# The last piece of an MLP's second matrix: seven products instead of eight for half of its columns, and one chunk of weights behind it

## The chip, the cores and the metric

The kernel runs on one core of a Trainium2 chip, in one launch. Its time is the device time in microseconds (us). Before the change three runs took 1203.53 us in the median (1203.21 to 1204.15). Five engines matter here: TensorE (PE, matrix products), VectorE (DVE) and ScalarE (ACT) for elementwise work, GpSimd (POOL) and SyncE (SP), which here only start transfers. Each engine works through its own instructions in the order in which the program holds them.

## The reference, cut to what matters

The kernel computes one layer of a decoder trunk for 256 tokens and 16 meta tokens, in float32. The change lies in its last part, the MLP:

```python
D_MODEL = 2048; SEQ = 256; D_FF = 8192
...
u = rms_norm(h, g_pre_mlp[l])
f = jnp.square(jax.nn.relu(u @ w_up[l])) @ w_down[l]
h = h + rms_norm(f, g_post_mlp[l])
return h[:, N_META:]
```

Call the activations A = relu(u @ w_up)^2 (256 tokens by 8192 features) and the weights B = w_down (8192 by 2048). The second matrix product is A @ B.

## The kernel before

**Pieces, halves, blocks.** The 8192 features are taken in NP = 8 pieces of 1024. Within a piece A falls into four blocks by token half t (128 tokens) and feature half h (512 features), and B into eight chunks by h and column block n (512 columns, n = 0 to 3). A chunk is 128 partitions by 4 by 512 numbers, 1 MB. Column blocks 2 and 3 ("X1" to "X4") are always computed plainly: each chunk is multiplied with the blocks of both token halves, and the sums stay in the PSUM banks `x00`, `x01`, `x10`, `x11` (column block, token half) over all pieces. Column blocks 0 and 1 (B11, B12, B21, B22) are computed by a scheme of seven products instead of eight (P1 to P7, the Strassen-Winograd form) in pieces 0 to 6. There each product takes one sum of B blocks and one sum of A blocks (a "form": A1 and A2 are the plain ones, S1 to S4 the sums). Its result lies in bank `a` or `b`, and `give` (L1697) adds it to one block of `F`, the sums of column blocks 0 and 1 in SBUF. In the last piece (i = NP - 1) these columns are computed plainly too, as Y1 to Y4.

**A product.** `down` (L1666 on) issues twelve matmuls of 512 columns, since each float32 number is split into a high and a low part: high by high, high by low, low by high, for four slices of the feature half.

**A chunk's way.** A 1 MB load on SP's queue brings it into one of five rooms (`raw_a`, `raw_c`, three `raw_m`; L1431). `split_raw` has ACT copy it to a high part (`hi`, L1475) and DVE subtract that to get the low part (`lo`, L1480). These parts have three slots in turn, so the split of a chunk starts only when the product three chunks earlier is done. A sum of two chunks is a DVE add in a room (L1496) or a load on POOL's queue that adds to what the room holds (`bring`, L1501). A room comes free after the last use of its chunk, and the next load waits for it.

**The order.** Everything is entered into a `Plan` with an engine, a cost and what it reads and writes. PE and SP keep the order of entry, and a slot of `hi` and `lo` is taken in turn. ACT and DVE take, of what can begin now, what is due first, by a due time worked back from the PE work that needs it; what no PE work needs has no due time and goes by entry. The order is fixed when the program is built. The PE order of the pieces is written out by hand; the last piece reads `Y1 U1b1 X1 Y3 Y2 Y4 X2 X3 X4`, where U1b1 is the last quarter of the product with w_up, from which the last activations come (`up_pair` L1545 on, `relu_squared`, `into_forms`).

**The end.** The last three chunks are not multiplied for both token halves in turn. After Y4 the code behind the loop runs X2, X3 and X4 for token half 0, then X2 for token half 1, then X3 and X4 for token half 1 in two column halves, into banks `a` and `b` (after a copy of `x11`, L1900). For each token half the output is F times g_post_mlp (`times_g`, L1883), the sum of squares on ACT (L969, in order of entry, as all write one scratch tile), a square root and a few small steps (`norm3`), and the last multiply-and-add with h1 (L1908), one per column stretch, each with its own output transfer.

```python
LAST_PIECE = "Y1 U1b1 X1 Y3 Y2 Y4 X2 X3 X4"
...
def last_of(w, s, t):
    h, n = AT[s]
    name, f = f"x{n - 2}{t}", (A1, A2)[t]
    plan.add("PE", 2.72, lambda: down(banks[name], split_at[w], h, f, False, h == 1),
             reads=half_names(w) + act_names(h, f), writes=(name,))
```

Of the kernel before, what the change touches and what calls it, by code (L numbers as in the profile page):

```python
# [14 lines left out]
P = 128  # L15
# [99 lines left out]
def hybrid_block(ctx: ExitStack, tc: tile.TileContext, ins: dict, out: bass.AP):  # L115
    nc = tc.nc
# [5 lines left out]
    NT = T // P  # L122
# [101 lines left out]
    NP = FF // PF  # L224
# [168 lines left out]
    for h in range(RH):  # L393
# [6 lines left out]
                        name=f"u_{tag}")[:, :, :, :L] for tag, n in (("um", KM), ("ux", KD - KM))], KM)  # L400
# [971 lines left out]
    NEXT = "X3 U0a0+ E2 U0a1+ X4 E1 P1 E3 E4 E5 U0b0+ P5 U0b1+ P3 P6 U1a0+ P7 U1a1+ P2 P4 U1b0+"  # L1372
    LAST_PIECE = "Y1 U1b1 X1 Y3 Y2 Y4 X2 X3 X4"
    steps = []
    for i in range(NP):
# [13 lines left out]

    BRINGS = {"P1": ("B11", "B12"), "E2": ("B12", "B22")}  # L1390

    SUMS_E = {"E1": ["T1"], "E3": ["T2", "T4", "T3"]}
    AT = {"B11": (0, 0), "B12": (0, 1), "B21": (1, 0), "B22": (1, 1),
          "Y1": (0, 0), "Y2": (1, 0), "Y3": (0, 1), "Y4": (1, 1),
          "X1": (0, 2), "X2": (1, 2), "X3": (0, 3), "X4": (1, 3)}
# [176 lines left out]
    def relu_squared(h, pr, i, s_name, box):  # L1572
# [17 lines left out]
        plan.add("ACT", 0.75, square, reads=(s_name,), writes=(s_name,))  # L1590
        if i < NP - 1 and h == 0:
            plan.add("ACT", 0.42, lambda: nc.scalar.copy(q_(S1Q), a_(A2)),
                     reads=(s_name,), writes=(f"q1{pr}",))
            plan.add("DVE", 0.42, lambda: nc.vector.tensor_sub(q_(S3Q), a_(A1), a_(A2)),
                     reads=(s_name,), writes=(f"q3{pr}",))
        elif i < NP - 1:
            plan.add("DVE", 0.42, lambda: nc.vector.tensor_sub(q_(S1Q), q_(S1Q), a_(A2)),
                     reads=(s_name, f"q1{pr}"), writes=(f"q1{pr}",))
            plan.add("DVE", 0.42, lambda: nc.vector.scalar_tensor_tensor(
                q_(S2Q), q_(S3Q), -1.0, a_(A2), op0=ALU.mult, op1=ALU.subtract),  # L1600
                reads=(s_name, f"q3{pr}"), writes=(f"q3{pr}",))
            plan.add("DVE", 0.42, lambda: nc.vector.tensor_add(q_(S4Q), a_(A1), q_(S2Q)),
                     reads=(s_name, f"q3{pr}"), writes=(f"q4{pr}",))
# [9 lines left out]
    def into_forms(h, pr, i, s_name, box):  # L1613
# [5 lines left out]
        def src():  # L1619
# [38 lines left out]
    for e, (s, i) in enumerate(steps):  # L1658
        if s[0] in "PEXY":
            last_reader[HALF_OF[s] if s in HALF_OF else AT[s][0], i] = e  # L1660
# [39 lines left out]
    def half_names(m_):  # L1700
        q = (first_n + m_) % 3
        return [f"hi{q}", f"lo{q}"]
# [18 lines left out]
    def product_plain(m_, s, i):  # L1721
        h, n = AT[s]
        for t, f in ((0, A1), (1, A2)):
# [4 lines left out]
                reads=half_names(m_) + act_names(h, f), writes=(name,))  # L1728


    LAST_BANK = {(0, 0): "a", (0, 1): "b", (1, 0): "u0", (1, 1): "u1"}

    def product_last(m_, s, i):
        h, n = AT[s]
        for t, f in ((0, A1), (1, A2)):
            name = LAST_BANK[n, t]
            plan.add("PE", 2.72, lambda t=t, f=f, name=name: down(
                banks[name], split_at[m_], h, f, h == 0, h == 1),
                reads=half_names(m_) + act_names(h, f), writes=(name,))
        for t in range(NT if h == 1 else 0):  # L1740
            name, blk = LAST_BANK[n, t], f"F{2 * t + n}"
            plan.add("DVE", 0.69, lambda t=t, name=name: nc.vector.tensor_add(
                F[:, t, n, :], F[:, t, n, :], banks[name]), reads=(name, blk), writes=(blk,))

# [88 lines left out]
    m_ = 0  # L1833
    tail = len(products) - 3
    for at_step[0], (s, i) in enumerate(steps):
# [17 lines left out]
        if s == "E3":  # L1853
            e3_at = m_
        {"U": product_up, "X": product_plain, "P": product_block, "Y": product_last,
         "E": product_e}[s[0]](m_, s, i)
# [131 lines left out]
```

## Time and profile before

| | |
|---|---|
| median of three runs | 1203.53 us |
| the profiled execution | 1202.46 us |
| its span in the profile | 1200.7 us |
| ACT busy | 650.9 us, 54% |
| POOL busy | 26.7 us, 2% |
| HBM read, written | 249.85 MB, 2.10 MB |

The span goes from the first to the last recorded instruction; the execution has 1.76 us around it. A row of the timeline gives the start in us from the start of the span, the duration, the engine, the line of the kernel, the operation, what it writes and reads, and in brackets how long the engine was idle before and on whom it waited. Since an instruction may start shortly before the one ahead of it on its engine has ended, what a row costs in a dense stretch is read from start to start. A row of the chain of waits gives the start, the time that this step took of the chain, and the engine and line.

### The profile page before, as it was taken

What the parts mean: (1) busy time and instruction counts of PE and PEld (TensorE: products, weight loads), DVE (VectorE), ACT (ScalarE), POOL (GpSimd) and SP (SyncE); (2) the same over time, 40 slices, a digit from 0 to 9 for tenths busy, and PEclk for the clock granted to TensorE, in tenths of its full rate; (3) what the DMA queues carried; (4) which work ended last, traced back from release to release, by engine and by line L of the source; (5) the groups of instructions that cost most, each with busy time, mean ns of one, the idle gap of its engine ahead of it and who ended that gap; (6) DMA issues with size and microseconds to landing.
All of it is one profiled execution on the core that took longest, in us unless ns stands there. A gap on an engine that the chain in (4) does not pass through costs nothing.

```text
span 1200.7 us, 16375 instructions
## 1 busy us (share of the span) xinstructions
PE 1191.2 (99%) x6694; PEld 1046.1 (87%) x6694; DVE 1015.0 (85%) x1128; ACT 650.9 (54%) x675; POOL 26.7 (2%) x37
## 2 busy tenths in 40 slices
PE   9999999999999999999999999999999999999997
PEld 9999988888888888898988888888889889888886
DVE  6899978999676778688898888898988988988966
ACT  6533344343584455666566565655665665565543
POOL 1000000000000000000000000000000000000000
PEclk9999999999999999999999999999999999999999
DMA  9655555556558578547777777786896787777851
GB/s 294 208 184 183 186 184 188 198 188 198 182 168 284 171 258 265 178 156 230 205 243 222 205 252 206 211 274 158 243 275 165 253 245 199 245 223 197 257 176 70
DMA packets 170043, 253.01 MB, mean 211 GB/s; under 512 B 4369, under 2 KB 92625, under 8 KB 169456
## 3 DMA queue, kind: packets, MB, share of 16 engines
q1 hardware_dynamic: 160000, 230.64, 58.6%
q0 software_dynamic: 9072, 20.08, 8.9%
q8 instruction: 52, 0.85, 0.3%
q10 hardware_dynamic: 896, 1.25, 0.3%
q14 instruction: 23, 0.19, 0.0%
HBM read 249.85 MB, written 2.10 MB: 210 GB/s over the span
## 4 chain that ended last, share of the span: by engine, by line
PE 99%; DVE 0%; DVEq 0%; ACT 0%; issue 0%; ACTq 0%
PE bank_u L485 18%; PE acc_gate L771 15%; PE bank_u L491 9%; PE acc_up L1673 8%; PE bank_a L1673 7%; PE o_c L1110 6%; PE bank_b L1673 6%; PE acc_z L480 4%; PE acc_co L771 4%; PE acc_po L771 4%; PE bank_b L1758 3%; PE acc_v L480 3%; PE acc_g L480 3%; PE acc_up L1758 3%; PE acc_vg L480 2%; PE acc_up L485 1%
## 5 line engine op out<-in xcount | busy, mean ns | idle before, releaser
L485 PE MATMUL bank_u<-m,hi 128*128 128x512 f32 x960 | 332.5, 391 | 0.0
L491 PE MATMUL bank_u<-m,lo 128*128 128x256 f32 x960 | 266.7, 278 | 0.0
L274 ACT CAST hi<-raw 128x2048 fp32r<-128x2048 f32 (+2 forms) x94 | 151.2, 1619 | 192.0 <-PE acc_gate L771 67.7
L1480 DVE TENSOR_TENSOR lo<-raw_m,hi 128x2048 fp32r<-128x2048 f32 (+1 forms) x98 | 208.8, 2137 | 44.6 <-ACT hi L1475 44.2
L1475 ACT CAST hi<-raw_m 128x2048 fp32r<-128x2048 f32 (+1 forms) x98 | 174.8, 1788 | 132.0 <-PE bank_u L485 61.8
L277 DVE TENSOR_TENSOR lo<-raw,hi 128x2048 fp32r<-128x2048 f32 (+2 forms) x94 | 180.1, 1925 | 40.5 <-ACT hi L274 39.9
L485 PEld LDWEIGHTS bank_u<-m,hi 128*128 128x128 f32 x960 | 180.3, 188 | 38.0
L491 PEld LDWEIGHTS bank_u<-m,lo 128*128 128x128 f32 x960 | 180.8, 188 | 1.4
L771 PE MATMUL acc_gate<-hi,u_um 128*128 128x512 f32 x416 | 131.5, 390 | 0.0
L546 DVE SCALAR_TENSOR_TENSOR c<-a,taps,c 128x256 f32<-128x256 f32 x240 | 115.6, 483 | 6.8
L771 PEld LDWEIGHTS acc_gate<-hi,u_um 128*128 128x128 f32 x416 | 78.1, 188 | 16.2
L1673 PE MATMUL acc_up<-hi,forms 128*128 128x512 f32 x272 | 86.8, 391 | 0.0
L1475 ACT CAST hi<-raw_c 128x2048 fp32r<-128x2048 f32 (+1 forms) x34 | 61.3, 1807 | 43.9 <-PE bank_u L485 24.5
L1480 DVE TENSOR_TENSOR lo<-raw_c,hi 128x2048 fp32r<-128x2048 f32 (+1 forms) x34 | 73.5, 2164 | 12.8 <-ACT hi L1475 12.7
L1480 DVE TENSOR_TENSOR lo<-raw_a,hi 128x2048 fp32r<-128x2048 f32 (+1 forms) x32 | 70.0, 2189 | 15.8 <-ACT hi L1475 15.8
L1475 ACT CAST hi<-raw_a 128x2048 fp32r<-128x2048 f32 (+1 forms) x32 | 58.5, 1832 | 44.6 <-PE bank_u L485 16.3
L1673 PE MATMUL bank_a<-hi,forms 128*128 128x512 f32 (+1 forms) x256 | 82.0, 383 | 0.0
L771 PE MATMUL acc_gate<-lo,u_um 128*128 128x512 f32 x208 | 80.9, 389 | 0.0
L1110 PE MATMUL o_c<-hi,m 128*128 128x512 f32 x208 | 65.5, 390 | 0.0
L1673 PE MATMUL bank_b<-hi,forms 128*128 128x512 f32 (+1 forms) x200 | 64.0, 383 | 0.0
L1673 PEld LDWEIGHTS acc_up<-hi,forms 128*128 128x128 f32 x272 | 51.1, 188 | 11.1
L1673 PEld LDWEIGHTS bank_a<-hi,forms 128*128 128x128 f32 x256 | 47.7, 188 | 9.5
(383 smaller groups left out, 2181.1 us busy)
## 6 DMA issues: line engine op xcount, KB each, us to landing
raw<-in_w_in_dram SPq DMA_DIRECT2D x52, 1024.0 KB, 5.1
raw_m<-in_w_down_dram SPq DMA_DIRECT2D x38, 1024.0 KB, 6.3
raw_m<-in_w_up_dram SPq DMA_DIRECT2D x37, 1024.0 KB, 6.0
raw_c<-in_w_down_dram SPq DMA_DIRECT2D x14, 1024.0 KB, 5.3
raw_a<-in_w_down_dram SPq DMA_DIRECT2D x12, 1024.0 KB, 6.0
raw_a<-in_w_up_dram SPq DMA_DIRECT2D x11, 1024.0 KB, 6.1
raw_o<-in_w_o_dram SPq DMA_DIRECT2D x10, 1024.0 KB, 7.1
raw_c<-in_w_up_dram SPq DMA_DIRECT2D x10, 1024.0 KB, 6.0
```

The source lines that it names most:

```text
L274: nc.scalar.copy(hi[:, sl, cs], raw[:, sl, cs])
L277: nc.vector.tensor_sub(lo[:, sl, cs], raw[:, sl, cs], f32(hi[:, sl, cs]))
L480: nc.tensor.matmul(acc, w[:, k[0], cs], act[:, k[1], a, off:], start=first and n == 0, stop=last and n == 2)
L485: nc.tensor.matmul(acc.rearrange("p (a t) -> p a t", a=2)[:, :, ts], hi[:, k[0], cs], act[:, k[1], :, off + ts.start:off + ts.stop], start ...
L491: nc.tensor.matmul(acc[:, :T], lo[:, k[0], cs], act[:, k[1], 0, off:], start=False, stop=stop, skip_group_check=True)
L546: nc.vector.scalar_tensor_tensor(c, conv["a"][:, q, i:i + T], taps[:, q, i:i + 1], c, op0=ALU.mult, op1=ALU.add)
L771: nc.tensor.matmul(acc, act(kk)[:, a_, ts_], w_[:, k, :], start=kk == 0 and n == 0, stop=kk == nk - 1 and n == 2)
L1110: nc.tensor.matmul(acc, form(k, a_), box[w_][:, k, :], start=start and k == 0 and n == 0, stop=stop and k == CK - 1 and n == 2, skip_group ...
L1475: nc.scalar.copy(box["hi"][:, ks, cs], raw[:, ks])
L1480: nc.vector.tensor_sub(box["lo"][:, ks, cs], raw[:, ks], f32(box["hi"][:, ks, cs]))
L1673: nc.tensor.matmul(acc, forms[h][:, f, k, a_, :], box[w_][:, k, cs], start=start and k == 0 and n == 0, stop=stop and k == KH - 1 and n == ...
L1758: nc.tensor.matmul(banks[bank][:, col_halves[half[1]]], forms[h][:, f, k, a_, :], split_at[m_][w_][:, k, cs], start=start and k == 0 and n ...
```

## The change

In the last piece column blocks 0 and 1 go by the seven products too. The PE order becomes `P1 U1b1 X1 X2 P5 X3 P6 P3 P7 P2 P4 X4`, and only X4 is left for the code behind the loop: X4 for token half 0, then X4 for token half 1 in two column halves. X2 and X3 are multiplied for both token halves inside the loop. The sums of A blocks (S1 to S4) are made in the last piece as in the others, and the sums of B chunks as well; where the other pieces add B22 to B12 at E2, the last piece, which has no E steps, does it at X3. `product_last` with its banks goes.

```diff
-    LAST_PIECE = "Y1 U1b1 X1 Y3 Y2 Y4 X2 X3 X4"
+    LAST_PIECE = "P1 U1b1 X1 X2 P5 X3 P6 P3 P7 P2 P4 X4"
...
-    BRINGS = {"P1": ("B11", "B12"), "E2": ("B12", "B22")}
+    BRINGS = {"P1": ("B11", "B12"), "E2": ("B12", "B22"),
+              ("X3", NP - 1): ("B12", "B22")}
...
-            if s in BRINGS:
-                to, what = BRINGS[s]
+            if (s, i) in BRINGS or s in BRINGS:
+                to, what = BRINGS.get((s, i)) or BRINGS[s]
...
-        if i < NP - 1 and h == 0:
+        if h == 0:
             plan.add("ACT", 0.42, lambda: nc.scalar.copy(q_(S1Q), a_(A2)),
...
-        elif i < NP - 1:
+        else:
             plan.add("DVE", 0.42, lambda: nc.vector.tensor_sub(q_(S1Q), q_(S1Q), a_(A2)),
...
-        if i == NP - 1:
-            return
...
-    def product_last(m_, s, i):
...
-    tail = len(products) - 3
+    tail = len(products) - 1
...
-    last_of(m_, "X2", 0)
     before_last(0)
-    ends = [(m_ + 1, "X3"), (m_ + 2, "X4")]
-    for w, s in ends:
-        last_of(w, s, 0)
+    last_of(m_, "X4", 0)
...
-    last_of(m_, "X2", 1)
     before_last(1)
...
     for e, cs in enumerate(col_halves):
-        for w, s in ends:
-            h = AT[s][0]
-            plan.add("PE", 1.36, lambda w=w, h=h, e=e, cs=cs: down(
-                banks["ab"[e]][:, cs], split_at[w], h, A2, False, h == 1, cs),
-                reads=half_names(w) + act_names(h, A2), writes=("ab"[e],))
+        plan.add("PE", 1.36, lambda e=e, cs=cs: down(
+            banks["ab"[e]][:, cs], split_at[m_], 1, A2, False, True, cs),
+            reads=half_names(m_) + act_names(1, A2), writes=("ab"[e],))
```

More of the change, by code (lines that the diff above doesn't have):

```diff
@@ L1388, in hybrid_block @@
     SUM_FOR = {"P6": ("B11", "B22"), "P4": ("B11", "B21")}
-    BRINGS = {"P1": ("B11", "B12"), "E2": ("B12", "B22")}
+    BRINGS = {"P1": ("B11", "B12"), "E2": ("B12", "B22"),
+              ("X3", NP - 1): ("B12", "B22")}
     SUMS_E = {"E1": ["T1"], "E3": ["T2", "T4", "T3"]}
     AT = {"B11": (0, 0), "B12": (0, 1), "B21": (1, 0), "B22": (1, 1),
-          "Y1": (0, 0), "Y2": (1, 0), "Y3": (0, 1), "Y4": (1, 1),
           "X1": (0, 2), "X2": (1, 2), "X3": (0, 3), "X4": (1, 3)}
@@ L1658, in hybrid_block @@
     for e, (s, i) in enumerate(steps):
-        if s[0] in "PEXY":
+        if s[0] in "PEX":
             last_reader[HALF_OF[s] if s in HALF_OF else AT[s][0], i] = e
@@ L1728, in product_plain @@
                 reads=half_names(m_) + act_names(h, f), writes=(name,))
-    LAST_BANK = {(0, 0): "a", (0, 1): "b", (1, 0): "u0", (1, 1): "u1"}
-    def product_last(m_, s, i):
[L1734 to L1743, printed above, removed]
     def product_block(m_, s, i):
@@ L1854, in hybrid_block @@
             e3_at = m_
-        {"U": product_up, "X": product_plain, "P": product_block, "Y": product_last,
+        {"U": product_up, "X": product_plain, "P": product_block,
          "E": product_e}[s[0]](m_, s, i)
```

## The prediction

> **What bounds the kernel now.** I read the page first (who is busy), then the chain of waits of the last 60 us (what sets the end), then VectorE's and ScalarE's timelines there, then transfers.
>
> ```profile
> PE 1191.2 (99%) x6694; PEld 1046.1 (87%) x6694; DVE 1015.0 (85%) x1128; ACT 650.9 (54%) x675; POOL 26.7 (2%) x37
> ```
>
> TensorE is without gaps; VectorE has 15% left over the kernel. The last piece in the chain of waits (the rows of U1b1, which lie between the first two here, left out):
>
> ```profile
> 1143.02 2.74 PE bank_a L1673 x12
> ...
> 1153.94 5.46 PE acc_up L1673 x24
> ...
> 1164.85 2.72 PE bank_a L1673 x12
> ...
> 1175.73 10.88 PE acc_up L1673 x48
> 1186.61 2.87 PE bank_a L1673 x24
> 1189.48 2.89 PE bank_b L1673 x24
> ```
>
> Twelve matmuls are 2.72 us; the same in two column halves half of 2.87 + 2.89, so 2.88. Y1 starts at 1143.02 and TensorE ends at 1192.37: sixteen products' worth at 2.72, two at 2.88, and a few hundredths. From there an end that TensorE has no part in runs to 1200.7. VectorE's timeline, from which all its prices come:
>
> ```profile
> 1123.51 2.29 DVE L1496 TENSOR_TENSOR raw_a<-raw_a,raw_c 128x2048 f32<-128x2048 f32 x1
> 1125.76 2.29 DVE L1480 TENSOR_TENSOR lo<-raw_c,hi 128x2048 fp32r<-128x2048 f32 x1
> 1127.97 0.68 DVE L1697 TENSOR_TENSOR F_raw<-F_raw,bank_a 128x512 f32<-128x512 f32 x1
> ...
> 1137.14 2.29 DVE L1480 TENSOR_TENSOR lo<-raw_m,hi 128x2048 fp32r<-128x2048 f32 x1
> ...
> 1139.95 0.68 DVE L1697 TENSOR_TENSOR F_raw<-F_raw,bank_a 128x512 f32<-128x512 f32 x1
> 1140.55 2.28 DVE L1480 TENSOR_TENSOR lo<-raw_m,hi 128x2048 fp32r<-128x2048 f32 x1
> ...
> 1158.40 0.69 DVE L1622 TENSOR_TENSOR forms<-pairs,forms 128x512 fp32r<-128x512 f32 x1
> ...
> 1166.83 2.29 DVE L1480 TENSOR_TENSOR lo<-raw_m,hi 128x2048 fp32r<-128x2048 f32 x1 [3.15 <-ACT hi L1475]
> ...
> 1171.05 0.43 DVE L1900 COPY bank_b<-acc_up 128x256 f32<-128x256 f32 x1
> 1171.39 0.68 DVE L1883 TENSOR_TENSOR F_raw<-F_raw,raw_m 128x512 f32<-128x512 f32 x1
> ...
> 1185.31 0.15 DVE L947 SCALAR_TENSOR_TENSOR v_mlp<-ssq_mlp,v_mlp 128x1 f32<-128x1 f32 x1
> ...
> 1186.57 0.75 DVE L1908 SCALAR_TENSOR_TENSOR F_raw<-F_raw,r_mlp,h 128x512 f32<-128x512 f32 x1
> ...
> 1188.04 0.15 DVE L938 TENSOR_REDUCE v_mlp<-ssq_mlp 128x1 f32<-128x3 f32 x1
> ...
> 1188.29 0.74 DVE L1908 SCALAR_TENSOR_TENSOR F_raw<-F_raw,r_mlp,h 128x512 f32<-128x512 f32 x1
> 1188.95 0.75 DVE L1908 SCALAR_TENSOR_TENSOR raw_m<-raw_m,r_mlp,h 128x512 f32<-128x512 f32 x1
> ...
> 1190.09 0.42 DVE L1943 TENSOR_TENSOR raw_m<-bank_a,raw_m 128x256 f32<-128x256 f32 x1 [0.39 <-ACT sq_last L1942]
> ...
> 1190.68 0.74 DVE L1908 SCALAR_TENSOR_TENSOR raw_m<-raw_m,r_mlp,h 128x512 f32<-128x512 f32 x1
> ...
> 1192.96 0.42 DVE L1943 TENSOR_TENSOR raw_m<-bank_b,raw_m 128x256 f32<-128x256 f32 x1 [1.53 <-ACT sq_last L1942]
> ...
> 1194.01 1.42 DVE L1908 SCALAR_TENSOR_TENSOR F_raw<-F_raw,r_mlp,h 128x384 f32<-128x384 f32 x2
> 1195.34 1.54 DVE L1908 SCALAR_TENSOR_TENSOR raw_m<-raw_m,r_mlp,h 128x512 f32<-128x512 f32 x3
> ```
>
> From start to start: a sum of two chunks 2.25; a low part 2.21; a `give` 0.60 (1139.95 to 1140.55), which I also take for `times_g` (same operation and size); a bank copy 0.34; `finish` 1.26; `start` 0.25; the end of a column half 0.59 and 1.05; an output step 0.66; the last five output steps 2.87 (1194.01 to 1196.88). After 1196.88 there are 3.82 us to the end: last transfers. Today token half 0 is finished (four output steps, the last at 1190.68) while TensorE still works.
>
> **What is removed.** Seven products for eight leave TensorE seventeen for eighteen, and of the split ones one remains: minus 2.88 us. Without stalls, in the chain's clock: P1 1143.02, U1b1 1145.77, X1 1151.22, X2 1156.68, P5 1162.12, X3 1164.84, P6 1170.28, P3 1173.00, P7 1175.72, P2 1178.44, P4 1181.16, X4 for half 0 1183.88, its halves 1186.60 to 1189.49.
>
> **What is added.** Three splits (twelve chunks for nine), sums for P6 and P4, two adding loads, sums of A blocks and their S1 to S4, seven `give` for four adds at L1742. The part up to X2 has room: P1 stands where Y1 stood, with the same chunk and slot, and the sums of A blocks made before it are those that every earlier piece makes there under a full TensorE. They cost nothing; if that cover went, each would cost its 0.60.
>
> **X2, moved forward.** It needs the forms of U1b1 and now starts 5.46 us after U1b1's end; Y2 had two chunks between. The steps as they ran before on ScalarE, U1b1 ending at 1153.94 in the chain:
>
> ```profile
> 1153.98 0.37 ACT L1552 COPY half<-bank_u 128x256 f32<-128x256 f32 x1 [2.35 <-PE bank_u L491]
> 1154.25 1.91 ACT L1475 CAST hi<-raw_m 128x2048 fp32r<-128x2048 f32 x1
> 1156.06 0.63 ACT L1582 ACTIVATE pairs<-pairs 128x512 f32<-128x512 f32 x1
> 1156.72 0.62 ACT L1621 CAST forms<-pairs 128x512 fp32r<-128x512 f32 x1
> ...
> 1164.88 1.91 ACT L1475 CAST hi<-raw_m 128x2048 fp32r<-128x2048 f32 x1 [3.53 <-PE bank_u L1673]
> ```
>
> The low form ended at 1158.40 + 0.69 = 1159.09, 5.15 us after U1b1, with a split ahead of it on both queues. That is 0.31 us early, and S1 to S4 are due later. X2's stall is bounded by 0 and by what P5's split, which takes the place of that split, can wait for its adding load:
>
> ```profile
> DMA to landing us min/median/max: 8.3/9.4/14.2
> ```
>
> That load starts when P1's low part is done, 1137.14 + 2.21 = 1139.35, as for Y1; median landing 1148.8, latest 1153.6. ScalarE gets to P5's split at 1151.5 and would hold the square behind it. By the median the stall is 0, by the latest 2.1 less 0.3, so 1.8. I take 0.
>
> **The run of products on VectorE.** A split starts when the product three chunks earlier ends; its low part starts 1.95 us later (1164.88 to 1166.83). Before X2's end VectorE has had all that is ready: the sum for P6, S1 to S4, X3's split. Then, each start the later of "high part ready" and "VectorE free": P6 low part 1164.10 (X2's end + 0.03 + 1.95), `give` P5 1166.31, P3 low 1166.91, sum for P4 1169.12 to 1171.37; P7 low must wait for X3's end, 1172.26 (0.89 idle); `give` P6 1174.47, P2 low 1175.07, `give` P3 1177.28, P4 low 1177.88, `give` P7 1180.09, X4 low 1180.69, `give` P2 1182.90 to 1183.50. Each low part is in time, and so is each `give` whose bank is written next: P6's by 1175.07 for P7 at 1175.72, P3's by 1177.88 for P2 at 1178.44, P7's by 1180.69 for P4 at 1181.16. The least margin is 0.47 us, so I put no stall on TensorE. But VectorE is full.
>
> **The end.** Where Y4 had X2, X3 and X4 behind it, the last F blocks are now whole only with P2 and P4. ScalarE squares each block ahead of its `times_g`, in order of entry, 0.75 apart:
>
> ```profile
> 1177.62 0.62 ACT L969 ACTIVATE ng_offset=None)_1_0_9569<-F_raw 128x512 f32<-128x512 f32 x1
> ...
> 1178.37 0.63 ACT L969 ACTIVATE ng_offset=None)_0_1_9585<-F_raw 128x512 f32<-128x512 f32 x1
> ```
>
> The first waits for `give` P2; from 1183.55 six squares end at 1184.30, 1185.05 and so on to 1188.05, each within hundredths of its `times_g` or ahead of it. VectorE: copy 0.34 to 1183.84; P4 ends at 1183.88, so `give` P4 1183.93 to 1184.53, the other copy to 1184.87 (both before the halves at 1186.60); five `times_g` to 1187.87; `start` 1188.12; `times_g` for X4's half 0 1188.72; `finish` 1189.98; `times_g` and `start` for half 1 1190.83; column half ends 0.59 and 1.05 to 1192.47, both of TensorE's long done; four output steps 2.64 to 1195.11; five 2.87 to 1197.98. With 3.82 behind: 1201.80, 1.10 us over 1200.7. What stood under three chunks of TensorE stands behind it: VectorE's work, not TensorE's end, sets the end.
>
> Gains of VectorE are bounded: without its idle 0.89 and 0.09 the end would be 1200.82, level with before. So no step of the order can earn the 2.88.
>
> **Transfers.** g_post_mlp's load waited for a room; P1's room is now held until P4, so the load moves behind P3's split, 1169.12.
>
> ```profile
> raw_m<-in_g_post_mlp_dram SPq DMA_DIRECT2D x1, 1024.0 KB, 4.5
> ```
>
> It lands at 1173.6, 11 us before use: free, under the splits. On SP's queue only it stands behind X4's load. The outputs of both halves now come in one go; their bytes, and the stretch in which the last ones go out today:
>
> ```profile
> HBM read 249.85 MB, written 2.10 MB: 210 GB/s over the span
> ```
>
> ```profile
> 1196.00:1198.00 2.00, 0.00 (x0) 0.00 (x0) 0.88 (x3) 0.00 (x0) 0.00 (x0) 0.50 0.87 327
> ```
>
> At 327 GB/s for a share of 0.87, full engines move 376 GB/s, and 2.10 MB takes 5.6 us. The outputs are issued over 1193.1 to 1198, about the same rate. Bounds: 0, if the queue keeps up; 0.7, if the whole 5.6 us runs before the last output's usual end starts to count (5.6 less the 4.9 of issue). I take 0.4, being near the edge.
>
> Sum: 1.10 + 0.4 = +1.5 us on the span, 1202.2. The profiled execution's 1202.46 (1.76 around the span) lies 1.07 below the median; I add the difference to the median: 1205.0.
>
> A rule weighed: two low parts in a row start 2.21 us apart though each row lasts 2.29. The Trainium skill, "VectorE: DVE Perf Modes", section "The DRAIN you can't avoid", says that the next operation does not start until the pipe is empty (and excepts, further on, one that is not held). Taken plainly, the 27 longer operations from 1172.26 on would each cost 0.08 more, an estimate of +2.2 us on top of the sum. The rows contradict it, so the sum keeps 2.21.
>
> **Rivals.** *TensorE alone counts* (chance 0.04). Everything new hides, as in pieces 0 to 6, and the time falls by 2.88 to 1200.65. For it: 99% busy, and scheme pieces without gaps. Against it: there U products of 5.44 us alternate with the P's, while here five P's stand in a row at 2.72 us with 2.21 + 0.60 of VectorE each. The Trainium skill, "Perfetto Trace Analysis", section "Identifying the Most-Contended Engine", would say this: optimize the engine with the highest occupancy first (it warns that matmul busy time flatters). It agrees with the row of 99%, and is not enough at the end.
>
> *X2 waits for its forms* (0.16): the adding load lands late, ScalarE's queue holds the square, 1.8 us of stall, after which VectorE's chain moves by as much: +3.3, 1206.8. It decides from a landing over 12.5 us after issue; the longest was 14.2, the median speaks against it.
>
> *A `give` behind a split* (0.17), the slower side: DVE's order puts a low part ahead of the `give` of the bank that the next product writes. TensorE then stands for 2.21 less the margin of about 0.5, so 1.7, and slots come free later, which VectorE pays as idle time. At two of the places P7, P2, P4: +3.4, in all +4.9, 1208.4. It decides from 0.47 us of lateness. Due times speak against it, the thin margin for it.
>
> *VectorE packs better* (0.05): no idle time, +0.5, 1204.0.
>
> **How the numbers follow.** The forecast itself has 0.58; its own range is 1203.6 (the gapless end) to 1206.3 (0.3 more of transfers, a microsecond of waits not seen). The whole range, 1203.3 to 1207.9, takes in the late load and leaves out the first rival and two thirds of the third, some 0.16. Below 0.2% (2.4 us) this kernel can't tell a change from none. Faster by more: 0.04. Slower by more than that, over 1205.9: both slower rivals, 0.33, and 0.11 of the forecast's own upper part, 0.44. Within: 0.52.
>
> **What would show it.** Right: TensorE's last matmul near 1189.5 with hardly a gap; VectorE without a gap over 0.9 us from 1164 to 1198; output steps of half 0 after the last column half; a longer stretch from TensorE's end to the span's end, near 12.7 instead of 8.3. X2 waiting for `forms`, or P7, P2, P4 for L1697, shows the rivals. Wrong would be an end after TensorE still near 8.3 us, or gaps in TensorE of over 2 us before 1162.

## The result and the profile after

| | before | after |
|---|---|---|
| median of 12 runs | 1203.49 us | 1206.22 us |
| lowest, highest | 1202.69, 1204.24 us | 1205.71, 1207.64 us |
| profiled execution, its span | 1202.46, 1200.7 us | 1205.85, 1204.1 us |

The ratio after to before is 1.0024, interval 1.0017 to 1.0032: 2.7 us slower, where 1205.0 us had been predicted with a range of 1203.3 to 1207.9. The spans differ by 3.4 us. Of these, 0.72 were there before the last piece began: P1 starts at 1143.74 in the chain of waits of after, where Y1 started at 1143.02. What is compared below is compared from there on, and there it is 60.36 us to the end for 57.68, so 2.68 us, as in the medians.

The busy line and the chain's shares on the page of after:

```profile
PE 1189.2 (99%) x6670; PEld 1042.9 (87%) x6670; DVE 1032.3 (86%) x1148; ACT 659.9 (55%) x684; POOL 29.2 (2%) x39
...
PE 97%; DVE 2%; DMA 0%; issue 0%; ACT 0%; SPq 0%; DVEq 0%; ACTq 0%
```

TensorE has 24 matmuls fewer and is still 99% busy; VectorE has 20 instructions and 17.3 us more. The shares hardly move. The chain of waits of after shows what did, in the last 45 us:

```profile
1143.74 2.75 PE bank_a L1671 x12
...
1151.94 10.92 PE acc_up L1671 x48
1162.88 1.93 ACT hi L1475
1164.83 2.29 DVE lo L1480
...
1176.61 2.98 PE bank_a L1671 x12
1179.59 2.80 PE bank_b L1671 x12
1182.39 2.81 PE bank_a L1671 x12
1185.23 0.70 DVE F_raw L1695
```

Before, this chain stayed on TensorE until its last matmul. Now it leaves TensorE at the end of X2 (1162.88) and goes by VectorE; P7, P2 and P4 are on it, but as links that wait for a `give` (L1695). From 1185.23 it never comes back to TensorE, though that works on until 1190.78. Behind TensorE's end lies this window (length, then the busy time and instructions of TensorE, weight loads, VectorE, ScalarE, GpSimd, then clock, DMA share and GB/s), first of before, then of after:

```profile
1192.40:1200.70 8.30, 0.00 (x0) 0.00 (x0) 3.81 (x10) 0.77 (x3) 0.00 (x0) 0.68 0.42 156
```

```profile
1190.80:1204.10 13.30, 0.00 (x0) 0.00 (x0) 8.94 (x26) 1.87 (x8) 0.00 (x0) 0.69 0.45 159
```

TensorE's end came 1.6 us sooner on each trace's own clock, and 5.0 us more lie behind it, nearly all of it VectorE's work (8.94 for 3.81 us).

TensorE's timeline of after, at the seams of the products (P5's first matmul, the last of P3 and the first of P7, the first of P2 and X4):

```profile
1162.68 0.39 PE L1671 MATMUL bank_b<-hi,forms 128*128 128x512 f32 x1
...
1176.05 0.39 PE L1671 MATMUL bank_b<-hi,forms 128*128 128x512 f32 x1
1176.61 0.47 PE L1671 MATMUL bank_a<-hi,forms 128*128 128x512 f32 x1 [0.16 <-DVE F_raw L1695]
...
1179.43 0.45 PE L1671 MATMUL bank_b<-hi,forms 128*128 128x512 f32 x1
...
1185.03 0.39 PE L1671 MATMUL acc_up<-hi,forms 128*128 128x512 f32 x1
```

Eight products' worth at 2.72 us from 1162.68 would put X4 at 1184.44; it starts at 1185.03, so 0.59 late. P7 is 0.33 late (P3's next matmul slot was 1176.28), and then each product takes 2.80 or 2.82. VectorE's timeline of after says why:

```profile
1167.04 0.68 DVE L1636 TENSOR_TENSOR forms<-F_raw,forms 128x512 fp32r<-128x512 f32 x1
...
1169.84 0.42 DVE L1602 TENSOR_TENSOR F_raw<-pairs,F_raw 128x256 f32<-128x256 f32 x1
...
1172.98 0.68 DVE L1636 TENSOR_TENSOR forms<-F_raw,forms 128x512 fp32r<-128x512 f32 x1
1173.58 2.28 DVE L1480 TENSOR_TENSOR lo<-raw_m,hi 128x2048 fp32r<-128x2048 f32 x1
1175.78 0.68 DVE L1695 TENSOR_TENSOR F_raw<-F_raw,bank_a 128x512 f32<-128x512 f32 x1
1176.38 2.28 DVE L1480 TENSOR_TENSOR lo<-raw_a,hi 128x2048 fp32r<-128x2048 f32 x1
1178.58 0.68 DVE L1695 TENSOR_TENSOR F_raw<-F_raw,bank_b 128x512 f32<-128x512 f32 x1
...
1185.23 0.69 DVE L1695 TENSOR_TENSOR F_raw<-F_raw,bank_a 128x512 f32<-128x512 f32 x1 [0.37 <-PE bank_a L1671]
...
1186.62 1.89 DVE L1866 TENSOR_TENSOR F_raw<-F_raw,raw_c 128x512 f32<-128x512 f32 x3
...
1189.92 0.16 DVE L938 TENSOR_REDUCE v_mlp<-ssq_mlp 128x1 f32<-128x3 f32 x1 [0.22 <-ACT ng_offset=None)_2_0_9665 L969]
...
1190.64 0.69 DVE L1866 TENSOR_TENSOR raw_m<-acc_up,raw_c 128x512 f32<-128x512 f32 x1 [0.37 <-ACT ng_offset=None)_3_0_9680 L969]
...
1194.75 1.41 DVE L1891 SCALAR_TENSOR_TENSOR F_raw<-F_raw,r_mlp,h 128x512 f32<-128x512 f32 x2
...
1198.72 1.53 DVE L1891 SCALAR_TENSOR_TENSOR raw_m<-raw_m,r_mlp,h 128x512 f32<-128x512 f32 x3
```

A low part and a `give` together take 2.80 us from start to start (1173.58 to 1176.38), a product 2.72. The `give` at 1175.78 ends at 1176.46 and P7 starts 0.15 later; those of 1178.58 and 1181.38 end at 1179.26 and 1182.06, and P2 and P4 start 0.17 behind each. From P7 on, TensorE goes at VectorE's pace. Behind 1185.23 lies one long queue of VectorE: copies, factors, roots, and from 1194.75 nine output steps, the last done at 1200.25. After that 3.85 us pass to the end, 3.82 before.

### The profile page after: what moved, and what is told of

The parts are those of the page before. It is cut to its first block, busy times and chain, and to the rows that moved or that the text cites. A ratio compares the mean times of both kernels' runs of the same rounds, so it can differ in the third digit from the quotient of the medians.

```text
span 1204.1 us, 16371 instructions
## 1 busy us (share of the span) xinstructions
PE 1189.2 (99%) x6670; PEld 1042.9 (87%) x6670; DVE 1032.3 (86%) x1148; ACT 659.9 (55%) x684; POOL 29.2 (2%) x39
## 4 chain that ended last, share of the span: by engine, by line
PE 97%; DVE 2%; DMA 0%; issue 0%; ACT 0%; SPq 0%; DVEq 0%; ACTq 0%
PE bank_u L485 18%; PE acc_gate L771 14%; PE bank_u L491 9%; PE acc_up L1671 7%; PE bank_a L1671 7%; PE o_c L1110 6%; PE bank_b L1671 5%; PE acc_z L480 4%; PE acc_co L771 4%; PE acc_po L771 4%; PE bank_b L1741 3%; PE acc_v L480 3%; PE acc_g L480 3%; PE acc_up L1741 3%; PE acc_vg L480 2%; PE acc_up L485 1%
## 5 line engine op out<-in xcount | busy, mean ns | idle before, releaser
L1475 ACT CAST hi<-raw_m 128x2048 fp32r<-128x2048 f32 (+1 forms) x101 | 180.5, 1792 | 132.1 <-PE bank_u L485 69.2
L1480 DVE TENSOR_TENSOR lo<-raw_m,hi 128x2048 fp32r<-128x2048 f32 (+1 forms) x101 | 215.6, 2141 | 38.5 <-ACT hi L1475 38.2
L1671 PE MATMUL acc_up<-hi,forms 128*128 128x512 f32 x280 | 89.4, 391 | 0.0
L1671 PE MATMUL bank_a<-hi,forms 128*128 128x512 f32 (+1 forms) x264 | 86.0, 387 | 0.2 <-DVE F_raw L1695 0.2
```

Source lines behind the costliest of these rows:

```text
L1475: nc.scalar.copy(box["hi"][:, ks, cs], raw[:, ks])
L1480: nc.vector.tensor_sub(box["lo"][:, ks, cs], raw[:, ks], f32(box["hi"][:, ks, cs]))
L1671: nc.tensor.matmul(acc, forms[h][:, f, k, a_, :], box[w_][:, k, cs], start=start and k == 0 and n == 0, stop=stop and k == KH - 1 and n == ...
```

## The experiments

The theory of the prediction, called A in the expectations: VectorE's queue behind the last `give` sets the end, with ScalarE's chain of squares close behind it. Against it stood A' (VectorE alone, ScalarE never in the way), B (TensorE or its inputs are late), C (the added work of the scheme costs the time, not the shortened cover) and D (only the length of the cover counts). The interval of a ratio is about 0.001 to each side, some 1.1 us, so single steps are read from the traces, and the times decide between theories that lie further apart. Each ratio is to the kernel before as it ran beside that row (medians of 1203.09 to 1203.49 us), so the ratios compare better than the medians. One measure returns below: from the start of `give` P4 to the first output step, 9.52 us in after (1185.23 to 1194.75). It is left blank where the run has no P4 or other products stand between the two.

| run | median us | ratio to before, interval | `give` P4 to the first output step on VectorE |
|---|---|---|---|
| after | 1206.22 | 1.0024, 1.0017 to 1.0032 | 9.52 |
| e1_no_factor | 1204.76 | 1.0012, 1.0003 to 1.0021 | 8.22 |
| e2_factor_twice | 1208.56 | 1.0044, 1.0031 to 1.0056 | 11.93 |
| e3_cover_alone | 1206.01 | 1.0024, 1.0015 to 1.0034 | |
| e5_two_behind | 1207.38 | 1.0035, 1.0022 to 1.0047 | |
| e4_squares_ready | 1205.52 | 1.0017, 1.0008 to 1.0025 | 8.74 |
| e6_factor_pool | 1205.00 | 1.0013, 1.0004 to 1.0022 | 8.26 |
| e7_pool_ready_act | 1203.76 | 1.0002, 0.9994 to 1.0011 | 7.09 |
| e9_outputs_too | 1204.57 | 1.0008, 1.0000 to 1.0017 | 9.29 |
| e10_forms_early | 1205.81 | 1.0020, 1.0011 to 1.0029 | 9.52 |
| e12_outputs_after_root | 1204.69 | 1.0011, 1.0003 to 1.0020 | 7.08 |
| e14_all_moves | 1204.08 | 1.0006, 0.9997 to 1.0015 | 7.04 |
| e15_all_but_outputs | 1203.36 | 0.9999, 0.9991 to 1.0008 | 7.03 |

### Less and more of VectorE's work behind the last product

Four of the eight factors with g_post_mlp (column blocks 0 and 1 of both token halves) are left out (e1_no_factor), or made twice, one of the two copies into a free room (e2_factor_twice).

```diff
-        plan.add("DVE", 0.69, lambda: nc.vector.tensor_mul(
+        plan.add("DVE", 0.69, lambda: n < 2 or nc.vector.tensor_mul(
```

> The changed kernel with four VectorE instructions left out: the products of F (column blocks 0 and 1, both token halves) with g_post_mlp, so these columns come out without that factor; the order of everything else is kept. Theory A (behind the last give, VectorE's queue sets the end, with ScalarE's chain of squares close behind it): 4 x 0.60 = 2.4 us of VectorE go, but the factor for X4's token half 0 cannot start before its square ends, which is seven squares after P2's give, about 1189.4 in the profile's clock instead of 1190.6; so about -1.2 us against the changed kernel, 1.0014 of the kernel before. Theory A' (VectorE's queue alone): -2.4 us, 1.0004. Theory B (the loss comes from TensorE, through X2's early place, the adding loads or stalls between the products): no change, 1.0022 to 1.0024.

```diff
+    spare = room_of[free_rooms[0]][:, :CW]
...
-        plan.add("DVE", 0.69, lambda: nc.vector.tensor_mul(
-            dst_of(t, n * CW, (n + 1) * CW), src, g_mlp[:, block(n)]),
+        def f():
+            if n < 2:
+                nc.vector.tensor_mul(spare, src, g_mlp[:, block(n)])
+            nc.vector.tensor_mul(dst_of(t, n * CW, (n + 1) * CW), src, g_mlp[:, block(n)])
+        plan.add("DVE", 0.69, f,
```

> The changed kernel with the same four VectorE products done twice, the first time into an unused room; the output is the reference's. Theories A and A': 4 x 0.60 = 2.4 us more in VectorE's queue behind the last give, all of it on the path: +2.4 us, 1.0044 of the kernel before. Theory B: no change, 1.0024.

Made twice: from `give` P4 to the output steps (1185.73 to 1197.66) 2.41 us more, and 2.3 us in the median (1206.22 to 1208.56). VectorE's timeline of this run:

```profile
1187.13 0.68 DVE L1869 TENSOR_TENSOR raw_a<-F_raw,raw_c 128x512 f32<-128x512 f32 x1
1187.91 0.69 DVE L1870 TENSOR_TENSOR F_raw<-F_raw,raw_c 128x512 f32<-128x512 f32 x1
1188.52 0.68 DVE L1869 TENSOR_TENSOR raw_a<-F_raw,raw_c 128x512 f32<-128x512 f32 x1
...
1193.31 0.15 DVE L938 TENSOR_REDUCE v_mlp<-ssq_mlp 128x1 f32<-128x3 f32 x1
```

The second factor of a pair starts 0.78 us behind the first (why it isn't 0.60, no run shows), so the row of factors takes 6.18 us (1187.13 to 1193.31) where the five of after take 3.01: 3.17 more, not 2.4. The waits for squares, 0.75 us of after's time there, are gone. VectorE's added work reaches the end, less the waits that it fills; that the rest equals the 2.4 us expected is luck. Left out: 1.30 us less there, 1.5 in the median, not 2.4. VectorE's timeline of the run without the four factors shows where the rest went:

```profile
1187.98 0.16 DVE L938 TENSOR_REDUCE v_mlp<-ssq_mlp 128x1 f32<-128x3 f32 x1 [1.32 <-ACT ng_offset=None)_2_0_9662 L969]
...
1188.70 0.69 DVE L1866 TENSOR_TENSOR raw_m<-acc_up,raw_c 128x512 f32<-128x512 f32 x1 [0.38 <-ACT ng_offset=None)_3_0_9676 L969]
```

VectorE now waits 1.32 and 0.38 us for ScalarE's squares, where it waited 0.22 and 0.37 in after: 1.11 more. With the 1.30 that makes 2.41, the four factors. So VectorE sets the end and ScalarE's chain is 1.3 us behind it; A' falls, and B as the cause of the whole.

### The cover alone

The kernel before, with its eight products and no scheme, but X2 and X3 inside the loop ahead of Y2 and Y4, so that only X4 lies behind (e3_cover_alone; the lines behind the loop change as in after).

```diff
-    LAST_PIECE = "Y1 U1b1 X1 Y3 Y2 Y4 X2 X3 X4"
+    LAST_PIECE = "Y1 U1b1 X1 Y3 X2 X3 Y2 Y4 X4"
...
-    tail = len(products) - 3
+    tail = len(products) - 1
...
```

> The kernel before with only the cover changed: eight plain products as before, but X2 and X3 moved into the loop ahead of Y2 and Y4 and only X4 left behind it (Y1 U1b1 X1 Y3 X2 X3 Y2 Y4 X4). No split, sum or form is added and TensorE has the same products. Theory A: TensorE ends where it did (1192.4), but token half 0 is finished behind it: finish at about 1192.2, then up to 5.1 us of VectorE before the last five output steps, which began at 1194.0: +2.4 to +3.3 us, 1.0020 to 1.0027. Theory C (the loss is the added splits, sums and forms, not the cover): within 0.5 us of before, 0.9996 to 1.0004.

The time is that of after (1206.01 us; 1.0024 in both), without a seven-product scheme in the last piece and with a TensorE that runs until 1192.5. VectorE's timeline of this run:

```profile
1184.24 0.69 DVE L1742 TENSOR_TENSOR F_raw<-F_raw,bank_u 128x512 f32<-128x512 f32 x1 [0.97 <-PE bank_u L1673]
...
1190.46 0.69 DVE L1883 TENSOR_TENSOR raw_m<-acc_up,raw_m 128x512 f32<-128x512 f32 x1 [0.90 <-ACT ng_offset=None)_3_0_9643 L969]
...
1194.57 1.41 DVE L1908 SCALAR_TENSOR_TENSOR F_raw<-F_raw,r_mlp,h 128x512 f32<-128x512 f32 x2
```

Here too all nine output steps come in one go, from 1194.57. The loss of cover is enough for the whole loss, and C falls as its cause. The queue ahead is not the same one, though: VectorE has some idle time here (0.97 for TensorE, 0.90 for a square) where after has more work. Counted from the start of the last piece, after has its last F block 2.13 us sooner (`give` P4 starts 41.49 us behind P1, the last add of L1742 here 43.62 behind Y1), and VectorE takes 1.91 us longer from there to the output steps (9.52 for 7.61). So the scheme's own work takes back what the saved product could have earned against this run. That the two come out equal to 0.2 us is in part chance.

### One chunk more behind the loop

The seven products in one row, X3 and X4 behind (e5_two_behind; the code behind the loop runs two chunks, and B22 is added to B12 at X2).

```diff
-    LAST_PIECE = "P1 U1b1 X1 X2 P5 X3 P6 P3 P7 P2 P4 X4"
+    LAST_PIECE = "P1 U1b1 X1 X2 P5 P6 P3 P7 P2 P4 X3 X4"
...
```

> The changed kernel with two chunks behind the loop instead of one: P1 U1b1 X1 X2 P5 P6 P3 P7 P2 P4, then X3 and X4 for token half 0, then for token half 1 in column halves; B22 is added to B12 at X2. Theory A with VectorE full already from P5 on (2.81 us per product of 2.72, and the sum for P4 and the low parts of S2 and S4 on top): TensorE waits 4 to 5 us in the run of products, ends near 1195 and has its 8.3 us behind it: -0.5 us against the changed kernel, give or take 1: 1.0012 to 1.0028. Theory D (only the length of the cover counts, the run of products has room): the saved product shows, 1.0004 or less, with no gap in TensorE over 1 us.

It came out slower than after, 1207.38 us. TensorE's timeline of this run, at the first matmuls of P3 and P7:

```profile
1169.49 0.47 PE L1671 MATMUL bank_b<-hi,forms 128*128 128x512 f32 x1 [1.14 <-DVE F_raw L1695]
...
1174.40 0.50 PE L1671 MATMUL bank_a<-hi,forms 128*128 128x512 f32 x1 [1.94 <-DVE F_raw L1695]
```

TensorE stands 1.14 and 1.94 us for a `give`. The first of these (started at 1168.66) comes behind the low parts of two chunks and of a form, the second (1173.66) behind a low part and a sum. X3 had been more than cover: its 5.44 us between P5 and P6 are where VectorE catches up. Without them the wait moves from the end into the row of products, which is the rival "a `give` behind a split" of the prediction, with 1.1 and 1.9 us at each of two places for the 1.7 estimated.

D falls, as far as it said that only the length of the cover counts. A missed too: it expected half a microsecond less than after, at most 1.0028, and 1.0035 was measured. Its 4 to 5 us of waits and TensorE's end near 1195 were about right (3.1 us in the two waits, the end at 1194.28). What it had wrong is the stretch behind that, 11.0 us to the end of the span (1205.3) instead of 8.3. VectorE's timeline of this run has all nine output steps behind TensorE again, so that the second chunk covers none of them:

```profile
1195.80 1.41 DVE L1891 SCALAR_TENSOR_TENSOR F_raw<-F_raw,r_mlp,h 128x512 f32<-128x512 f32 x2
```

### Moving VectorE's work: order and other engines

Squares and factors entered in the order in which their blocks become whole (e4_squares_ready):

```diff
-        sum_of_squares(t, NB - 2)
-        times_g(t, NB - 2)
...
-    for t in range(NT):
-        for n in range(NB - 2):
-            sum_of_squares(t, n)
-            times_g(t, n)
+    for t, n in ((0, 2), (1, 2), (0, 1), (1, 1), (0, 0), (1, 0)):
+        sum_of_squares(t, n)
+        times_g(t, n)
```

> The changed kernel with the squares and factors entered in the order in which their blocks become whole (X2's blocks first, then F after P3, P7, P2, P4) instead of by token half; the work is the same. Theory A (VectorE's queue with ScalarE's chain of squares close behind it): only the waits of VectorE on that chain go (0.22 and 0.37 us in the changed kernel's timeline): -0.5 us against the changed kernel, 1.0020 of before. If the chain of squares were the bound itself, moving five of seven squares ahead would give -1.2 us or more, 1.0014 or less.

The four factors on GpSimd (e6_factor_pool):

```diff
-        plan.add("DVE", 0.69, lambda: nc.vector.tensor_mul(
+        engine, mul = ("POOL", nc.gpsimd) if n < 2 else ("DVE", nc.vector)
+        plan.add(engine, 1.5 if n < 2 else 0.69, lambda: mul.tensor_mul(
```

> The changed kernel with the four factors of F (column blocks 0 and 1) computed by POOL instead of VectorE, the order of squares as in the changed kernel. Theory A: as when they are left out, about -1.2 us against the changed kernel, 1.0014 of before, since the chain of squares then ends last. Rival: VectorE and POOL get in each other's way, or POOL's product lasts over 2 us, and little or nothing is won: 1.0020 to 1.0030.

Both together, and the two bank copies of L1883 on ScalarE (e7_pool_ready_act):

```diff
-        plan.add("DVE", 0.42, lambda e=e, cs=cs: nc.vector.tensor_copy(
+        plan.add("ACT", 0.42, lambda e=e, cs=cs: nc.scalar.copy(
```

> Three moves together on the changed kernel: the four factors on POOL, squares and factors in the order in which blocks become whole, the two bank copies on ScalarE. Theory A: VectorE has 3.1 us less behind the last give and no chain of squares before it; the factor of X4's half 0 then follows its square at about 1188.6 in the changed kernel's clock instead of 1190.6, and the run of nine output steps starts at 92.2 to 92.5 instead of 94.75: -2.4 us, 1.0004 of before. If only one of queue and chain bound the end, no more than the -1.2 us of one of them.

From `give` P4 to the output steps these three take 8.74, 8.26 and 7.09 us for 9.52, and the times follow: 1205.52, 1205.00, 1203.76. The readiness order alone removes the waits of 0.22 and 0.37 us for a square. The factors on GpSimd, 2.4 us of VectorE's work, earn 1.26 there; GpSimd's and VectorE's timelines of that run:

```profile
1186.13 5.05 POOL L1867 TENSOR_TENSOR F_raw<-F_raw,raw_c 128x512 f32<-128x512 f32 x4 [30.69 <-ACT ng_offset=None)_0_0_9639 L969]
```

```profile
1189.61 0.15 DVE L938 TENSOR_REDUCE v_mlp<-ssq_mlp 128x1 f32<-128x3 f32 x1
...
1190.05 1.15 DVE L947 SCALAR_TENSOR_TENSOR v_mlp<-ssq_mlp,v_mlp 128x1 f32<-128x1 f32 x1
```

The one-column step at 1190.05 takes 0.15 us in after; here it ends at 1191.20, with GpSimd's last factor (1186.13 + 5.05 = 1191.18). A microsecond of the gain is lost there. The 1.2 us expected came about, but not for the reason given: VectorE waits for no square here, and what holds up the root of half 0 is GpSimd's last factor. With all three moves the four factors start on GpSimd at 1182.56, under the products, and the kernel is level with before.

### Output steps on two engines

The run with all three moves, and the two output steps of token half 0 with columns below 1024 as a scaling on ScalarE and an addition on GpSimd. In the first form (e9_outputs_too) a scaling may run as soon as the root of half 0 is there, in the second (e12_outputs_after_root) only behind both roots.

```diff
+            names = [f"out{t}{b}" for b in range(c0 // CW, (c1 - 1) // CW + 1)]
+            if t == 0 and c1 <= D // 2:
+                def add(dst=dst, c0=c0, c1=c1):
+                    nc.gpsimd.tensor_add(dst, dst, h1[:, t, c0:c1])
+                    nc.sync.dma_start(ov[:, t, c0:c1], dst)
+                plan.add("ACT", 0.62, lambda dst=dst: nc.scalar.activation(
+                    dst, dst, AF.Copy, scale=norm3.r[:, t]), reads=[f"r{t}"], writes=names)
+                plan.add("POOL", 1.3, add, reads=names)
+                continue
```

> The same three moves, and the output steps of token half 0 for column blocks 0 and 1 taken off VectorE as well: ScalarE multiplies by the root, POOL adds h1. Theory A: two output steps less in VectorE's last run, 2 x 0.66: -1.3 us more than with the three moves, -3.7 us against the changed kernel, 0.9993 of before, which beats both kernels by showing 1.2 us of the saved product. Rival: POOL's share is slow (over 2 us each) or TensorE's end with its chain (8.3 us behind 1190.8 in the changed kernel's clock) binds first: not under 0.9998.

```diff
-                    dst, dst, AF.Copy, scale=norm3.r[:, t]), reads=[f"r{t}"], writes=names)
+                    dst, dst, AF.Copy, scale=norm3.r[:, t]), reads=["r0", "r1"], writes=names)
```

> The run with the outputs of half 0 off VectorE (column blocks 0 and 1, ScalarE times root, POOL plus h1), with ScalarE's two multiplications entered behind the last square, which they delayed by 1.24 us. Theory A: two of VectorE's nine last output steps are gone and nothing is delayed, so 1.3 us less than with the three moves alone: 0.9992 of before. Rival (port): in the run before, a VectorE step of 0.15 us took 1.23 while POOL added; if VectorE and POOL really shut each other out, VectorE's last run stretches by as much as it saves: 1.0002 or more.

Both were to be faster than before; they took 1204.57 and 1204.69 us, 0.8 and 0.9 more than the run without it (1203.76). The intervals overlap, but the traces say the same: VectorE's last output step ends 0.89 and 0.74 us later, counted from the start of P1. In the first the scalings stood ahead of the last square, and VectorE waited for that; its timeline:

```profile
1192.68 0.42 DVE L1928 TENSOR_TENSOR raw_m<-bank_b,raw_c 128x256 f32<-128x256 f32 x1 [1.24 <-ACT sq_last L1927]
1193.02 1.23 DVE L1938 SCALAR_TENSOR_TENSOR half_v<-last_ssq,half_v 128x1 f32<-128x1 f32 x1
```

In the second that wait is gone and the output steps start at 1192.28, 7.08 us behind `give` P4, but they are longer. VectorE's timeline, then GpSimd's:

```profile
1192.28 2.41 DVE L1899 SCALAR_TENSOR_TENSOR raw_m<-raw_m,r_mlp,h 128x512 f32<-128x512 f32 x2
...
1195.94 2.58 DVE L1899 SCALAR_TENSOR_TENSOR raw_m<-raw_m,r_mlp,h 128x512 f32<-128x512 f32 x3
```

```profile
1192.33 1.81 POOL L1891 TENSOR_TENSOR F_raw<-F_raw,h 128x512 f32<-128x512 f32 x1 [3.20 <-ACT F_raw L1893]
1195.93 1.26 POOL L1891 TENSOR_TENSOR F_raw<-F_raw,h 128x512 f32<-128x512 f32 x1 [1.78 <-ACT F_raw L1893]
```

Two and three output steps take 2.41 and 2.58 us where they took 1.41 and 1.53, each beside an addition of GpSimd. Taking 1.32 us (two steps) off VectorE cost it 2.05 elsewhere. The rival of the expectation, that the two engines get in each other's way, held.

### The forms earlier, and everything together

The low parts of S3, S2 and S4 with earlier due times in the last piece (e10_forms_early):

```diff
-            split_form(0, S3, "S3", S3Q, "q3")
+            split_form(0, S3, "S3", S3Q, "q3", 12.0 * (i == NP - 1))
...
-            split_form(1, S2, "S2", S2Q, "q3")
-            split_form(1, S4, "S4", S4Q, "q4")
+            split_form(1, S2, "S2", S2Q, "q3", 4.0 * (i == NP - 1))
+            split_form(1, S4, "S4", S4Q, "q4", 6.0 * (i == NP - 1))
...
-    def split_form(b, f, name, q, q_name):
+    def split_form(b, f, name, q, q_name, late=0.0):
...
```

> The changed kernel with the low parts of S2, S3 and S4 made due earlier in the last piece (an allowance of 4, 12 and 6 us in the plan), so that S3 is split before U1b1 and the sums for S2 and S4 directly after it; the work is the same. In the changed kernel S2's and S4's low parts and one sum (1.54 us) stand among the splits behind X2's end, and P7 waits. If that is the cause of the 0.6 us by which TensorE and the last give are late, they come 0.5 to 0.7 us earlier: -0.6 us against the changed kernel, 1.0019 of before. Rival: VectorE has no room earlier either, the work only pushes other splits: no change, 1.0024.

P7's low part now follows the sum for P4 directly, at 1173.01. TensorE's timeline in this run, at the first matmuls of P5, P7 and X4:

```profile
1162.44 0.39 PE L1671 MATMUL bank_b<-hi,forms 128*128 128x512 f32 x1
...
1176.04 0.46 PE L1671 MATMUL bank_a<-hi,forms 128*128 128x512 f32 x1
...
1184.46 0.39 PE L1671 MATMUL acc_up<-hi,forms 128*128 128x512 f32 x1
```

P7 starts five products behind P5 (13.60 us), without a wait. X4 starts 22.02 us after P5 for 22.35 in after; the 0.26 over eight products that remain are the three periods of 2.80. The start of `give` P4 is 0.33 us nearer to that of P1 than in after, about half of the 0.6 expected. The time, 1205.81 us, can't be told from that of after.

Then all moves, with the output steps on two engines (e14_all_moves) and without (e15_all_but_outputs); in both the last factors also wait for the squares of their block, and the root of half 0 is entered ahead of that half's last factor.

```diff
-            reads=(name, f"raw{room_g}"), writes=(f"out{t}{n}", name if n < 2 else f"raw{room_f}"))
+            reads=(name, f"raw{room_g}") + (f"ssq{t}{n}",) * (n == NB - 1),
+            writes=(f"out{t}{n}", name if n < 2 else f"raw{room_f}"))
...
-    times_g(0, NB - 1)
     plan.add("DVE", 1.5, lambda: norm3.finish(0), reads=("v0", f"ssq0{NB - 1}"), writes=("r0",))
+    times_g(0, NB - 1)
```

> All moves on the changed kernel: factors on POOL, squares by readiness, bank copies on ScalarE, outputs as in the run with the multiplications behind the last square, the forms due earlier, and token half 0's root ahead of its last factor. Theory A: 0.6 us less than without the last two moves, 0.9987 of before, which beats both kernels. Rival (port): 0.9998 or more.

> The same without touching the outputs: all nine output steps on VectorE; factors on POOL, squares by readiness, bank copies on ScalarE, forms due earlier, root ahead of the last factor. Theory A: 0.6 us less than with the three moves alone, from TensorE's earlier end: 0.9997 of before.

With the output steps shared 1204.08 us (1.0006, where 0.9987 was expected; the rival held again), without 1203.36, which is the time of before to within the interval (0.9999, 0.9991 to 1.0008). GpSimd's and VectorE's timelines of the latter:

```profile
1179.30 2.46 POOL L1867 TENSOR_TENSOR F_raw<-F_raw,raw_c 128x512 f32<-128x512 f32 x1 [24.90 <-ACT ng_offset=None)_1_0_9600 L969]
```

```profile
1181.11 2.79 DVE L1480 TENSOR_TENSOR lo<-raw_m,hi 128x2048 fp32r<-128x2048 f32 x1
...
1191.45 1.40 DVE L1890 SCALAR_TENSOR_TENSOR F_raw<-F_raw,r_mlp,h 128x512 f32<-128x512 f32 x2
```

The output steps start at 1191.45, 2.8 us sooner than in after, counted from the start of P1. One low part, which begins while GpSimd's first factor still runs (until 1181.76), takes 2.79 us for 2.29. None of these versions was faster than the kernel before. The saving of 2.88 us on TensorE is about what the four output steps of half 0 cost (4 x 0.66), which before stood under TensorE's last matmuls; no run moves these four steps alone, so that this is an estimate.

## Why the prediction was right

The direction, the mechanism and the range held. Point by point:

- *The end is set by VectorE, not TensorE*: shown, by the chain that leaves TensorE at X2, by the window of 13.3 us behind TensorE (12.7 predicted), and by the factors made twice, whose time came through but for the waits that it filled. The rival "TensorE alone counts" fell.
- *X2 doesn't wait*: right. The chain has X1 and X2 as one row, 10.92 us for 48 matmuls, without a gap. The load of the rival landed in time: ScalarE's split for P5 began at 1152.24, directly behind its copy for U1b1 (1151.97).
- *No stall of TensorE in the row of products*: nearly right; the idle time was 0.16 us, and 0.59 us of lateness in all. The margins of about half a microsecond were used up, and the rival of a `give` behind a split showed in a small form here and in full when X3 was taken out of the row.
- *g_post_mlp's load is hidden*: right. SP issued it at 1169.95, it landed 4.8 us later, and its first use is at 1186.62.

The size was off: +1.5 us forecast, +2.7 measured. The terms of the sum, from P1's start on, in us:

| term | predicted | measured |
|---|---|---|
| VectorE's queue as in the working (the same by construction, since the rows below are counted against it) | 1.10 | 1.10 |
| late `give` P4 | 0 | 0.58 |
| `give` P4 to the output steps, beyond the 8.54 of the working | 0 | 0.98 |
| output steps (5.51) | 0 | -0.01 |
| last transfers | 0.4 | 0.03 |
| sum | 1.5 | 2.68 |

So what the sum had at nothing came to 1.56 us. The forecast's own range had allowed for one microsecond of waits not seen and 0.3 more of transfers; 1206.22 still lies within it, 0.1 under its upper end, because the 0.4 for transfers did not come. That is luck in part.

*The step that failed first* is "before X2's end VectorE has had all that is ready: ... S1 to S4". Part of that work came later: the low parts of S2 and S4 and one sum, at 1167.04, 1169.84 and 1172.98, together 0.60 + 0.34 + 0.60 = 1.54 us in the row of products, where the working had 0.89 of idle time for it. Less the 0.89, that is 0.65, and P7's low part began 0.60 late. S2's sums wait for S3's split, because both use one room, and in the last piece only P7 needs S3, so its due time is late. With earlier due times P7 no longer waited, and `give` P4 was 0.25 late instead of 0.58. The row was also counted at TensorE's 2.72 us a product; once VectorE is behind, it goes at VectorE's 2.80.

*The second* is "ScalarE squares each block ahead of its `times_g`". For the first of the blocks that are still in a bank of PSUM the order was the other one. ScalarE's timeline of after:

```profile
1189.20 0.60 ACT L969 ACTIVATE ng_offset=None)_2_0_9665<-acc_up 128x512 f32<-128x512 f32 x1 [1.32 <-DVE raw_m L1866]
```

The square stood 1.32 us for the factor that reads the same bank, and then VectorE stood for the square, 0.22 and 0.37 us; `start` (L938) begins at 1189.92, 0.29 behind five factors of 0.60 from 1186.62, and the next factor 0.72 later where 0.25 was counted, 0.76 us in both places. Another 0.45 lies ahead of the first factor, 1.39 us behind the start of `give` P4 (1185.23 to 1186.62) where the working had 0.94: one of the two copies of L1883 was to fill the idle time ahead of that `give`, and both came behind it. The roots and the column halves were 0.23 shorter. With the readiness order the stretch was 8.74 us, near the 8.54 of the working. The Trainium skill, "PSUM — Partial Sum Buffer", section "PSUM bank collisions raise a hardware error", says that two engines may not access one bank in the same 32 partitions at the same time, two readers included, so that programs have to order such reads; the trace is in line with it, with the square 0.09 us behind the factor's end (1188.43 + 0.68 = 1189.11), and a working that has two engines read one bank should put them one behind the other.

*The third* is the 0.4 us for transfers, by which the outputs of both halves were to back up. The last output step ends 3.85 us before the end, 3.82 in before. In the runs whose output steps stayed on VectorE, this time lay between 3.8 and 4.4 us, so that a trace can't show a few tenths here; in after the queue kept up.

The two rules that the prediction weighed: low parts still start less than their length apart (2.20 us for 2.28 at 1173.58), so the sum's 2.21 was the right price. And the engine with the highest occupancy was the wrong one to follow: TensorE lost 2.88 us of products, stayed at 99%, and the kernel became slower.

The 0.72 us by which the last piece begins later in the trace of after lie within the scatter of single executions: in the chains of waits of e1 and e2, which differ from after only behind the last `give`, P1 starts at 1143.07 and 1144.22. Whether the forms' due times alone earn anything stays open. In that trace the last output step ends 0.32 us sooner, counted from P1, but 4.41 us lie behind it instead of 3.85, and the medians differ by less than their interval.

## What to carry to other kernels

At the end of a kernel, a product saved on the fullest engine is worth only what the queue behind it gives back: count, for each part of the output, the vector work that comes after its last input, and compare it with the matrix work that is still to run beside it. What lies between the products can be cover as well; taking a pause out of a dense row moves the wait to where it was. And work moved to an idle engine is checked against what that engine shares with the full one.

## What the runs showed of the hardware

VectorE steps that read two operands from SBUF wait for a running GpSimd operation: 0.15 us became 1.15 and 1.23 (e6, e9), and two output steps went from 1.41 to 2.41 (e12). While GpSimd's factors ran in e6, a reduction with one operand stayed at 0.15 us (L938 at 1189.61), and two factors with one operand in PSUM at 1.29. It goes the other way too: under VectorE's low parts the four factors on GpSimd took 6.94 us (e7) for 5.05 (e6). The Trainium skill, "SBUF — State Buffer", section "Who interferes with whom", describes this: the second SBUF input of a VectorE instruction comes through a read port shared with GpSimd, and who issues first holds it. The traces agree. The price for VectorE was about 1 us where most of a GpSimd operation on 128x512 (1.26 us) was still to run, and 0.50 us in e15, where 0.65 us of it were left.
